# Accumulating transfers in contiguous rows, one addition of the value halves per pair of heads, and a written DMA order behind the attention

## Chip, cores and metric

The kernel runs on one core of one Trainium2 chip. The metric is the device time of one execution in microseconds. The core has a matrix engine (PE, with its own queue for weight loads, PEld), three engines for elementwise work (DVE, ACT, and the Pool, also called GpSimd), and SP, which here only issues DMAs. Each engine takes its instructions in order and waits on semaphores. An instruction that issues a DMA takes its place in the queue of the engine that issues it. All plain transfers are issued by SP (a few by ACT); those that add to their destination are issued by the Pool.

## What is computed

One hybrid decoder block with 16 meta tokens ahead of 1024 tokens of 1024 channels:

```python
h = rmsnorm(x, norm_g)
proj = jnp.einsum('bld,dn->bln', h, w_in)
u_pool, z_pool, q, k, v, z_attn, f_logit, g_pool, g_attn = jnp.split(proj, _split_points(), axis=-1)
y_pool = causal_multiscale_pool(u_pool, pool_w, pool_scale) * jax.nn.silu(z_pool)
log_f = jax.nn.log_sigmoid((f_logit + b_forget).astype(jnp.float32))
y_attn = forgetting_attention(q, k, v, log_f).reshape(B, L, ATTN_WIDTH) * jax.nn.silu(z_attn)
merged = (jax.nn.sigmoid(g_pool) * jnp.einsum('blc,cd->bld', y_pool, w_up_pool)
          + jax.nn.sigmoid(g_attn) * jnp.einsum('blc,cd->bld', y_attn, w_up_attn))
return x + jnp.einsum('bld,de->ble', merged, w_out)
```

A last RMS norm follows and the meta tokens are dropped. The pooling has four groups of 128 channels with windows of 2, 4, 8 and 16 positions. The attention has eight heads of 64 channels, is causal, and carries a decay that is summed from the forget gates.

## The kernel before, in words

Every float32 product is made from three products of rounded numbers: each operand is split into a high part (a rounded copy, written by ACT) and a low part (the rest, a subtraction on the DVE or the Pool), and high x high, high x low and low x high are added in PSUM.

**Start.** The tokens are normalised, transposed and split into `hh` and `hl`, four tensors in the pool `hp`, two for each half of the channels. They stay in SBUF until the end of product 1 below.

**Attention** (the class `Unit` and the loop over `units`, from line 777). There are 16 units: four pairs of heads, two heads each, two halves of 512 queries. A unit goes over five or nine blocks of 128 keys: products, maximum, exponent, split of the probabilities, product with the values. Heads use both halves of the 128 PSUM rows: the values' high parts give one half of 64 rows and their low parts the other, so the sum of the two halves is the result. `Unit.finish` (from line 733) copies the 128 rows to SBUF (line 737), stores the high half to `sp_y` in device memory (line 739, on SP) and adds the low half to the same place with an accumulating DMA (line 740, on the Pool). The softmax sums go to `sums` (line 745). Between these steps the PE is given filling work: the projections of queries, keys and values of the next pair, and of the gates, whose results go to device memory (line 336). The PE's order is written by hand; ACT, DVE, Pool and SP are ordered by a scheduler.

**Sums in device memory.** Two products of 1024 x 1024 matrices are made by Strassen's scheme with seven products of 512 x 512 blocks. It needs sums and differences of blocks, and these are made beside the attention by DMAs: `put` (line 578) copies, `add` (line 581) is an accumulating DMA of the Pool, behind the last sum of the softmax on that engine. `TD` are the sums for `w_out`, `GS` those for the weights of the two gates, `HS` those for the activations. `SUMS` (line 609) lists what is issued after which unit. A block has 512 rows of 512 numbers.

**The gates' products** (lines 866 to 1111). Seven products, numbered 0 to 6, of 48 matmuls each (`g_prod`, line 944; four row blocks of 12), give `za` and `zp`, the gates of the two branches. Product n needs its weights loaded (`w_in_`) and split (`w_split`, lines 929 and 931: ACT, then the Pool), and, from product 2 on, its activations loaded (`h_in`) and split (`h_split`, lines 937 to 942: ACT, then the DVE). Products 0 and 1 read `hh` and `hl` themselves; the split activations of the later ones lie in the pool `hq`, which takes over the space of `hp`. Sums of two products are made by the DVE (`plus_`, line 963) or by accumulating in the same bank. Between the products stand:

- `pool_chain` (line 865): the load of a pooling group `u` and its windowed sums on the DVE, two to five instructions; `pool_split` (line 886) splits the result; `pool_mm` (line 829) applies the 128 x 128 map.
- `sums_in` (line 893): the softmax sums are loaded, added, inverted and stored to `recs`.
- `attn_in` (line 845) loads the attention's result `y`; `attn_norm` (line 850) loads the reciprocal sums `rc`, spread over 64 rows, and multiplies.

From the first product on, the order of PE, ACT, DVE and Pool is the written one (line 980); SP is still ordered by the scheduler. The pool with tag `g` has 13 buffers of 4 KB and serves all these loads.

**Up and out.** Then the pooled and attended values are multiplied with the two up projections (32 groups of 12 matmuls, their results multiplied with the gates at line 1090), and the last Strassen product with `w_out` (line 1203) and the final norm follow.

## Time and profile before

| | us |
|---|---|
| median of three runs | 773.66 (773.03 to 774.5) |
| the profiled execution | 771.57 |
| its span | 769.8 |
| PE busy | 727.8 (95% of the span) |
| DVE busy | 538.6 (70%) |
| ACT busy | 416.9 (54%) |
| Pool busy | 352.4 (46%) |

The page of the profile gives each engine's busy time, the DMA queues, and groups of instructions by line. A row of a group names the line, the engine, the operation, the tile written and the tiles read, the count, the busy time and the mean in ns, and last the idle time of the engine just ahead of them and what ended it. The windows view gives the same busy times for a stretch of the span. The chain of waits goes back from the last instruction, at each step to what released it. In the timeline a row has start, length, engine, line and operation, and in brackets the idle time ahead and what ended it.

The stages by the trace: the attention from 26 to 487 us, the last filling work until 498.7, products 0 and 1 until 520.6, products 2 to 5 until 571.2, product 6 with the pooling maps until 599.4, the up projections until 686.4, the output product and the last norm until the end.

### The profile page before, as it was taken

The page shows a single profiled execution, that of the slowest core. Times are in us where ns is not written, and L with a number is a line of the kernel's source. Part 1 is how long each engine was busy: PE and PEld are TensorE (multiplying, and loading weights), DVE is VectorE, ACT ScalarE, POOL GpSimd, SP SyncE. Part 2 cuts the span into 40 slices and gives each one's busy share as a digit, 9 for nine tenths or more (in the row PEclk, how much of TensorE's full clock was granted, in tenths as well). Part 3 has the DMA queues.
Part 4 walks back from the last instruction along what each step waited for, and adds up shares of the span by engine and source line. Part 5 has one row for each costly group of instructions (what it writes and reads, how often), then busy time and mean ns, then how long its engine had stood idle before and what let it go on. Part 6 is the DMA issues. An engine that isn't in the chain of part 4 may idle for free.

```text
span 769.8 us, 10843 instructions
## 1 busy us (share of the span) xinstructions
PE 727.8 (95%) x3637; PEld 619.5 (80%) x3637; DVE 538.6 (70%) x913; ACT 416.9 (54%) x914; POOL 352.4 (46%) x430
## 2 busy tenths in 40 slices
PE   9999999998999989998999989999867999999996
PEld 6988989996797778887888878887755888888885
DVE  5643668697688787887878778408566744787775
ACT  7753566664676457665665466136444623535355
POOL 5422148656446585453654577347733001004343
PEclk9999999998999999999999999999997999999999
DMA  9111214957955949448373883735932547673005
GB/s 305 44 29 28 66 57 133 224 169 149 212 135 109 261 84 210 107 92 210 72 165 116 210 193 99 222 125 218 321 90 84 189 155 231 217 280 103 0 1 219
DMA packets 89866, 114.16 MB, mean 148 GB/s; under 512 B 11249, under 2 KB 54257, under 8 KB 89730
## 3 DMA queue, kind: packets, MB, share of 16 engines
q1 hardware_dynamic: 79840, 94.07, 38.7%
q0 software_dynamic: 8672, 16.78, 14.0%
q10 hardware_dynamic: 1298, 2.63, 0.9%
q8 instruction: 28, 0.46, 0.2%
q14 instruction: 28, 0.23, 0.1%
HBM read 87.04 MB, written 48.43 MB: 176 GB/s over the span
## 4 chain that ended last, share of the span: by engine, by line
PE 60%; DVE 16%; ACT 8%; issue 6%; DMA 3%; POOL 1%; POOLq 0%; SPq 0%; DVEq 0%; ACTq 0%
PE pj L164 35%; PE pj L1203 8%; PE pj L948 6%; DVE pl L714 4%; DVE S L709 2%; PE po L730 2%; PE pt L1203 2%; PE pt L948 2%; ACT S L678 2%; ACT S L710 2%; DVE m L685 1%; PE ps L669 1%; PE ps L670 1%; DMA hraw<-hs 1%; ACT ph L713 1%
## 5 line engine op out<-in xcount | busy, mean ns | idle before, releaser
L164 PE MATMUL pj<-hh,whi 128*128 128x512 f32 (+3 forms) x640 | 146.4, 356 | 0.4 <-DVE V L304 0.4
L164 PE MATMUL pj<-hl,whi 128*128 128x512 f32 (+3 forms) x640 | 145.1, 356 | 0.0
L164 PE MATMUL pj<-hh,wlo 128*128 128x512 f32 (+3 forms) x640 | 144.1, 352 | 0.0
L152 POOL TENSOR_TENSOR wlo<-raw,whi 128x256 fp32r<-128x256 f32 x116 | 94.9, 941 | 97.5 <-ACT whi L150 48.0
L164 PEld LDWEIGHTS pj<-hl,whi 128*128 128x128 f32 x640 | 110.7, 193 | 12.5
L164 PEld LDWEIGHTS pj<-hh,whi 128*128 128x128 f32 x640 | 109.5, 191 | 12.4 <-PE pj L294 0.6
L164 PEld LDWEIGHTS pj<-hh,wlo 128*128 128x128 f32 x640 | 108.9, 190 | 11.7
L714 DVE TENSOR_TENSOR pl<-S,ph 128x512 fp32r<-128x512 f32 (+4 forms) x112 | 98.1, 888 | 22.4 <-ACT ph L713 21.5
L722 POOL TENSOR_TENSOR acc<-acc,S 128x272 f32<-128x272 f32 (+4 forms) x80 | 77.7, 971 | 8.4 <-ACT S L710 2.8
L678 ACT ACTIVATE S<-ps,negc 128x400 f32<-128x400 f32 (+2 forms) x96 | 48.5, 514 | 57.4 <-DVE S L676 52.6
L685 DVE TENSOR_TENSOR m<-m,S 128x272 f32<-128x272 f32 (+4 forms) x80 | 52.4, 655 | 23.2 <-ACT S L678 21.1
L136 POOL TENSOR_TENSOR gw<-graw,gw 128x256 fp32r<-128x256 f32 x48 | 48.5, 1065 | 28.9 <-ACT gw L929 28.9
L710 ACT ACTIVATE S<-S 128x512 f32<-128x512 f32 (+4 forms) x112 | 49.2, 478 | 19.6 <-DVE S L709 19.5
L948 PE MATMUL pj<-gh,gw 128*128 128x512 f32 x180 | 45.0, 403 | 13.8 <-DVE zp L963 10.0
L713 ACT ACTIVATE ph<-S 128x512 fp32r<-128x512 f32 (+4 forms) x112 | 52.0, 478 | 4.4 <-PE po L730 4.1
L948 PEld LDWEIGHTS pj<-gh,gw 128*128 128x128 f32 x180 | 34.4, 194 | 23.4 <-issue 10.4
L709 DVE TENSOR_TENSOR S<-S,pt 128x512 f32<-128x512 f32 (+4 forms) x112 | 50.7, 498 | 0.6
L669 PE MATMUL ps<-qa,ka 128*128 128x512 f32 (+4 forms) x112 | 38.0, 340 | 9.9 <-ACT S L678 9.9
L730 PE MATMUL po<-pl,V 128*128 128x512 f32 (+4 forms) x112 | 38.6, 345 | 7.4 <-DVE pl L714 6.8
L1090 DVE TENSOR_TENSOR rl<-pj,rl 128x512 f32<-128x512 f32 x32 | 22.0, 690 | 30.4 <-PE pj L164 30.4
L150 ACT ACTIVATE whi<-raw 128x512 fp32r<-128x512 f32 x58 | 33.9, 622 | 14.0 <-PE pj L164 7.6
L720 POOL TENSOR_TENSOR acc<-S 128x400 f32<-128x400 f32 (+1 forms) x16 | 20.2, 1266 | 39.0 <-ACT S L710 39.0
(227 smaller groups left out, 1351.7 us busy)
## 6 DMA issues: line engine op xcount, KB each, us to landing
raw<-in_w_in_dram SPq DMA_DIRECT2D x31, 512.0 KB, 5.9
xt<-in_x_dram SPq DMA_DIRECT2D x8, 512.0 KB, 6.4
sp_gp<-st SPq DMA_DIRECT2D x16, 256.0 KB, 4.2
gs<-in_w_in_dram POOLq DMA_DIRECT2D x4, 1024.0 KB, 10.1
td<-in_w_out_dram POOLq DMA_DIRECT2D x4, 1024.0 KB, 12.1
sp_ga<-st SPq DMA_DIRECT2D x16, 256.0 KB, 2.7
graw<-gs SPq DMA_DIRECT2D x8, 512.0 KB, 5.2
rl<-sp_gp SPq DMA_DIRECT2D x8, 512.0 KB, 4.2
```

The source lines that it names most:

```text
L152: ins = nc.gpsimd.tensor_tensor(lo[:, k:k + 2], raw[:, k:k + 2], r32(hi[:, k:k + 2]), op=ALU.subtract)
L164: nc.tensor.matmul(ps, a, b, start=(i == 0), stop=(i == len(seq) - 1))
L678: nc.scalar.activation(s[:kb, f0:], ps[:kb, f0:], AF.Identity, bias=nb_)
L685: nc.vector.tensor_tensor(m[:kb, c0:], m[:kb, c0:], s[:kb, c0:], op=ALU.max)
L709: nc.vector.tensor_tensor(s[:kb, c0:], s[:kb, c0:], self.pm[:kb, c0:], op=ALU.subtract)
L710: exps.append(nc.scalar.activation(s[:kb, c0:], s[:kb, c0:], AF.Exp))
L713: nc.scalar.activation(ph[:kb, c0:], s[:kb, c0:], AF.Copy)
L714: dves.append(nc.vector.tensor_tensor(pl[:kb, c0:], s[:kb, c0:], r32(ph[:kb, c0:]), op=ALU.subtract))
L722: accs.append(nc.gpsimd.tensor_tensor(acc[:kb, c0:], acc[:kb, c0:], s[:kb, c0:], op=ALU.add))
L730: nc.tensor.matmul(self.po[:, c0:], v, r[:kb, c0:], start=(b == 0 and i == 0), stop=(b == self.nb - 1 and i == 1))
L948: nc.tensor.matmul(ps, op_w[n][p][k // 2][:, k % 2, i * 128:(i + 1) * 128], op_h[n][q][k // 2][:, k % 2], start=start and m == 0, stop=m = ...
L1203: nc.tensor.matmul(ps, pick(A_, k, p)[:, i * 128:(i + 1) * 128], pick(B_, k, q)[:, c0:c1], start=start and n == 0, stop=n == 11, skip_grou ...
```

## The change

Four things are changed.

1. **Form of the additions.** An accumulating transfer of a block goes as 128 rows of 2048 numbers (8 KB) between contiguous blocks in place of 512 rows of 512 (2 KB). So that both sides are contiguous blocks of device memory, the low parts of `hl` and the second summands in the weights are first copied there (`l11`, `l22`, `GS[5]`, `TD[5]`), and the list `SUMS` is written anew. It has 14 accumulating transfers as before, and 15 plain entries (four of them for the blocks of `hh` and `hl`) in place of 11.
2. **Value halves.** A unit stores both halves, to `sp_y` and `sp_y2`. `add_y(p)` adds the two blocks of a pair of heads with one accumulating transfer. It is issued after units 5, 9 and 13 for the first three pairs, and behind the attention for the last.
3. **Order behind the attention.** From product 0 on, SP's order too is the written one. The loads get functions of their own (`u_in`, `rc_in`, `sums_in` parted from `sums_out`) and stand earlier. The chains of groups 2 and 1 stand ahead of product 1, that of group 0 between the first sums behind it; `h_split(2)` and `h_split(3)` stand together; `attn_norm(0)` and `(1)` come together, the other two a product earlier each. A tile of 4 KB that is never read is added to the pool `hq`.
4. **One part of a split on the DVE.** In `w_split` for products 3 to 6 the last of the four subtractions is made by the DVE.

The core of the diff:

```diff
     def add(dst, src):
-        after(nc.gpsimd.dma_start(dst, src, accum_op=ALU.add), accs[-1])
+        d, r = [t.rearrange("(p k) c -> p (k c)", k=4) for t in (dst, src)]
+        after(nc.gpsimd.dma_start(d, r, accum_op=ALU.add, max_dma_last_dim=8192), accs[-1])
...
     def put_h(n):
         put(rows_of(HS[n]), hblock(hh4, n))
-
-    def add_h(n):
-        add(rows_of(HS[n]), hblock(hl4, n))
+        put(rows_of(HS["l" + n]), hblock(hl4, n))
...
+    def add_y(p):
+        d, r = [spill[n, p].rearrange("(p k) c -> p (k c)", k=2) for n in ("y", "y2")]
+        after(nc.gpsimd.dma_start(d, r, accum_op=ALU.add, max_dma_last_dim=8192), accs[-1])
...
-            yd = spill["y", self.p][hr, self.q0:self.q0 + 512]
-            nc.sync.dma_start(yd, t[hr])
-            after(nc.gpsimd.dma_start(yd, t[lr], accum_op=ALU.add), accs[-1])
+            for n, part in (("y", hr), ("y2", lr)):
+                nc.sync.dma_start(spill[n, self.p][hr, self.q0:self.q0 + 512], t[part])
...
         sums_of(i)
+        if i % 4 == 1 and i > 1:
+            add_y(i // 4 - 1)
...
+    def rc_in(p):
+        RC[p] = rc = gp.tile([128, SEQ], F32, name="rc", tag="g")
         for e in range(2):
...
+    def attn_norm(p):
+        nc.vector.tensor_tensor(Y[p], Y[p], RC[p], op=ALU.mult)
...
-            pool_tt(lo[k][:, c], raw_w[n][k][:, c], r32(hi[k][:, c]), ALU.subtract)
+            tt(lo[k][:, c], raw_w[n][k][:, c], r32(hi[k][:, c]), ALU.subtract,
+               nc.vector if n > 2 and k and c else nc.gpsimd)
...
+    add_y(3)
     w_in_(1)
-    next(cg[3])
+    u_in(3)
     h_in(2)
     w_in_(2)
+    u_in(2)
     for k in range(2):
         w_split(1, k)
-    run(cg[3])
+    run(pool_chain(3))
     M2 = ExitStack()
-    M2.enter_context(tc.manual_schedule(engines={mybir.EngineType.PE, mybir.EngineType.Activation,
-                                                 mybir.EngineType.DVE, mybir.EngineType.Pool}))
+    M2.enter_context(tc.manual_schedule())
+    sums_in()
     prods(ga_, 0, True)
+    u_in(1)
+    u_in(0)
     h_in(3)
+    sums_out()
...
     w_in_(3)
-    sums_in()
+    run(pool_chain(2))
+    run(pool_chain(1))
     prods(gb_, 1, True)
     HX.close()
...
-    h_split(2)
-    next(cg[2])
-    next(cg[2])
-    plus_(za[0][:, T0_], gb_[0])
-    next(cg[2])
-    plus_(za[1][:, T0_], gb_[1])
-    run(cg[2])
-    plus_(za[2][:, T0_], gb_[2])
     attn_in(0)
     attn_in(1)
+    rc_in(0)
+    h_split(2)
+    h_split(3)
+    c0_ = pool_chain(0)
+    for i in range(3):
+        plus_(za[i][:, T0_], gb_[i])
+        next(c0_, None)
+    w_in_(4)
+    hq.tile([128, SEQ], F32, name="pad", bufs=1)
+    h_in(4)
+    rc_in(1)
+    attn_in(2)
+    attn_in(3)
 
     prods(ga_, 2, False)
-    h_split(3)
     for k in range(2):
         w_split(3, k)
     plus_(za[3][:, T0_], gb_[3])
-    w_in_(4)
-    h_in(4)
-    run(cg[1])
+    w_in_(5)
+    h_in(5)
     for i in range(4):
         keep(zp[i][:, T0_], ga_[i])
     attn_norm(0)
-    attn_in(2)
+    attn_norm(1)
+    rc_in(2)
+    rc_in(3)
```

Behind products 3 and 4 the loads `w_in_(6)` and `h_in(6)` go one product earlier, chain 0 leaves its place behind product 3, `attn_norm(2)` and `(3)` go one product earlier, and `pool_split` and the first step of chains 0 to 2 lose a written dependency on an earlier instruction of the same engine.

More of the change, by code (lines that the diff above doesn't have):

```diff
@@ L137, in pool_tt, with tt @@
         return ins
+    def tt(out, x, y, op, eng):
+        if eng is nc.gpsimd:
+            pool_tt(out, x, y, op)
+        else:
+            eng.tensor_tensor(out, x, y, op=op)
     los = []
@@ L875, in pool_chain @@
             add = nc.vector.tensor_tensor(n[:, lo + step:], s[:, lo + step:], s[:, lo:L - step], op=ALU.add)
-            if not i:
+            if g == 3 and not i:
                 after(add, last_dve)
@@ L1022, in tile_hybrid_block @@
     h_split(4)
-    w_in_(5)
-    h_in(5)
+    w_in_(6)
+    h_in(6)
     pool_split(3)
@@ L1028, in tile_hybrid_block @@
     pool_split(2)
-    run(cg[0])
     keep(zp[2][:, T1_], gb_[2])
     keep(zp[3][:, T1_], gb_[3])
-    attn_norm(1)
-    attn_in(3)
+    attn_norm(2)
     prods(gb_, 4, False)
@@ L1038, in tile_hybrid_block @@
     h_split(5)
-    w_in_(6)
-    h_in(6)
     pool_split(1)
@@ L1044, in tile_hybrid_block @@
         silu(zp[i][:, T0_], zp[i][:, T0_], -1.0)
-    attn_norm(2)
+    attn_norm(3)
     prods(ga_, 5, False, (3, 2, 1, 0))
```

75 lines of the change are left out of this document (36 added, 39 removed).

## The prediction

> **What bounds the kernel now.** I read the page first, then the windows cut at the borders of the stages, then the chain of waits from 500 to 600 us, then who waited for whom in that stretch. The page and the DMA view:
>
> ```profile
> span 769.8 us, 10843 instructions
> DMA packets 89866, 114.16 MB, mean 148 GB/s; under 512 B 11249, under 2 KB 54257, under 8 KB 89730
> sp_y<-t SPq DMA_DIRECT2D x16, 128.0 KB, 3.2
> ```
>
> The windows (first pair: length and PE busy, the last three: granted clock, DMA share, GB/s):
>
> ```profile
> core 0: us, PE busy (x) PEld busy (x) DVE busy (x) ACT busy (x) POOL busy (x), PEclk, DMA share, GB/s
> 26.00:487.00 461.00, 442.88 (x2354) 386.24 (x2353) 349.31 (x655) 273.16 (x679) 246.03 (x288) 0.99 0.55 132
> 487.00:520.60 33.60, 33.60 (x150) 27.69 (x149) 4.83 (x6) 8.86 (x12) 12.09 (x17) 1.00 0.58 187
> 520.60:571.00 50.40, 45.52 (x193) 35.45 (x192) 37.10 (x32) 26.84 (x32) 34.45 (x29) 1.00 0.70 230
> 571.00:599.40 28.40, 18.39 (x74) 14.68 (x73) 17.09 (x22) 13.82 (x22) 9.19 (x12) 0.82 0.32 99
> 599.40:686.40 87.00, 87.00 (x385) 72.03 (x384) 55.07 (x82) 35.19 (x49) 5.72 (x8) 1.00 0.64 216
> ```
>
> The kernel is bound by the PE nearly everywhere, so a change can only pay where the PE stands still. In the attention that is 461.0 - 442.9 = 18.1 us, spread over 16 units. From 599.4 to 686.4 it is nothing. Between 520.6 and 599.4 it is 4.9 + 10.0 = 14.9 us in a sixth of the attention's time, and this is the stage that the change rewrites. Ahead of it, from 487 to 520.6, the PE is full while the DVE works 4.8 us of 33.6. The chain through the stage (start, length, what):
>
> ```profile
> 509.84 8.16 PE pj L948 x36
> 518.00 2.73 PE pt L948 x12
> ...
> 571.19 1.39 PE pj L164 x6
> 572.86 3.96 DMA rc<-recs
> ...
> 578.04 0.69 DVE zp L963
> 578.75 1.82 ACT zp L960 x3
> 581.13 0.69 DVE wlu L1069
> 581.82 0.61 DVE zp L963
> 582.57 4.39 PE pj L948 x12
> ...
> 588.35 2.74 PE pj L948 x12
> ```
>
> An undisturbed product of 48 matmuls takes 8.16 + 2.73 = 10.9 us. Products 2 to 5 start at 520.7 and end at 571.2: 50.5 us where 4 x 10.9 = 43.6 would do, so 6.9 us go in small waits. Then the PE runs six matmuls of the pooling map (1.39 us) and stands from 572.6 to 582.6, since product 6 adds to a bank that the DVE reads last at L963. In that gap an add of L963, queued on the DVE behind a normalisation waiting for `rc`, comes at 578.0, and a second one ends at 582.4. The 12 matmuls after the gap take 4.39 us, the next 12 take 2.74: 1.65 us more. So the stage holds 6.9 + 10.0 + 1.65 = 18.6 us above the PE's own work.
>
> The DVE is what it waits for. Its waits from 487 to 600 us (total, times, longest), and its groups from 520.6 to 600:
>
> ```profile
> DVE gh L940 <- ACT gh L937: 21.4, 2, 12.2
> DVE y L855 <- DMA rc<-recs: 9.4, 2, 7.2
> DVE y L855 <- DMA y<-sp_y: 2.4, 1, 2.4
> ```
>
> ```profile
> L942 DVE TENSOR_TENSOR gh<-hraw,gh 128x1024 fp32r<-128x1024 f32 x8 | 11.2, 1446 | 2.3 <-ACT gh L937 2.3
> L890 DVE TENSOR_TENSOR pll<-u,plh 128x1024 fp32r<-128x1024 f32 x4 | 6.2, 1562 | 1.6 <-ACT plh L889 1.6
> ...
> L882 DVE SCALAR_TENSOR_TENSOR u<-s,u 128x1024 f32<-128x1024 f32 x3 | 4.5, 1501 | 0.1
> L875 DVE TENSOR_TENSOR s<-u 128x1039 f32<-128x1039 f32 x3 | 4.2, 1411 | 0.0
> ...
> L875 DVE TENSOR_TENSOR s<-s 128x1037 f32<-128x1037 f32 x2 | 2.8, 1422 | 0.1
> ...
> L875 DVE TENSOR_TENSOR s<-s 128x1033 f32<-128x1033 f32 x1 | 1.2, 1225 | 0.0
> ```
>
> It stands 21.4 us for `gh` of product 2, then has all pool chains but one (12.7 us) in the crowded part, and there waits another 11.8 us for `rc` and `y` transfers. The SP row says why they come late:
>
> ```profile
> 538.55 1.12 SPq L854 DMA_DIRECT2D rc<-recs  x2
> ```
>
> **The change part by part.**
>
> *Pool chains 2 and 1 ahead of product 1, chain 0 between the first sums.* Three chains are nine instructions, 4.5 + 4.2 + 2.8 + 1.2 = 12.7 us. Chain 0 is one L875 and one L882, 1.41 + 1.50 = 2.9 us. The other seven, chains 2 and 1, move into the 21.4 us in which the DVE stood: 9.8 us. Their loads (`u_in`) stand ahead of h_in(3) on SP and land while the PE is full. Cover: products 0 and 1, 21.8 us long. Chain 0 stays past 520, but ahead of the work that was late.
>
> *h_split(2) and (3) together, with a padding tile.* Eight tiles of the pool `hq` lie on the space of the transposed activations; the pad is meant to put them on the half that product 0 reads (8 x 4,096 bytes fit in two tensors of 17,408, if they start at the same byte). If so, their low parts (one left of h_split(2), two of h_split(3) at 1.45) run during product 1 too: about 4.3 us more out of the crowded part. If not, they wait for product 1 as now; with chains 2 and 1 out of the way that costs the PE under 1 us.
>
> *rc and y loads.* The store of `recs` is followed by the loads y0, y1, rc0 and only then by w_in_(4), where SP stands until product 1 has left the space; behind that stand h_in(4), rc1, y2, y3. So rc0 goes out before product 1 is over, the rest right behind it, where the first two loads of `rc` now go out at 538.6; attn_norm(0) stands behind the last low part and six short instructions, about 525 by the sums above. I take the 11.8 us of DVE waiting as gone; if rc1 (behind two loads of 1 MB) is late by 4 us, that lies under product 2, which ends at 531.6.
>
> *Four parts of w_split from the Pool to the DVE.* A 128x512 addition is 0.69 us (L963 above): 2.8 us more on the DVE. On the Pool, the splits of products 3 to 6:
>
> ```profile
> 501.31 8.40 POOL L136 TENSOR_TENSOR gw<-graw,gw 128x256 fp32r<-128x256 f32 x12 [2.04 <-ACT gw L929]
> ```
>
> ```profile
> L136 POOL TENSOR_TENSOR gw<-graw,gw 128x256 fp32r<-128x256 f32 x16 | 11.5, 811 | 2.0 <-ACT gw L929 2.0
> L740 POOL DMA_DIRECT2D sp_y<-t x1 | 0.8, 842 | 11.3 <-DMA sp_y<-t 11.3
> L136 POOL TENSOR_TENSOR gw<-graw,gw 128x256 fp32r<-128x256 f32 x32 | 37.0, 1192 | 26.8 <-ACT gw L929 26.8
> ```
>
> (The first fence is the Pool's timeline; in the second the first two rows are of 487 to 520.6, the third of 520.6 to 600.) Six instead of eight at 1.19 us are 7.2 us per product of 10.9, so the Pool keeps up. The moved chains now run beside the first group: at worst its 16 become 1192 ns each, 6 us later, ending near 516 instead of 501.3 + 8.4 = 509.7 and still ahead of product 2.
>
> *add_y(3)* is the one wait that is new on the Pool. Behind it stand the splits of product 1. But the accumulating transfer in its place now already makes the Pool wait 11.3 us, for a store of the same unit: no change.
>
> The DVE so gains 9.8 + 4.3 + 11.8 - 2.8 = 23.1 us, more than the 14.9 the PE lost: something else is late next. For products 2 to 5 I find nothing, since their splits wait for the product two before. They end at 520.7 + 43.6 = 564.3, the six matmuls at 565.7. For product 6 it is the ACT and DVE pair that starts when product 4 leaves its tiles, at 520.7 + 32.7 = 553.4. The ACT rows for it:
>
> ```profile
> 566.72 1.99 ACT L937 ACTIVATE gh<-hraw 128x1024 fp32r<-128x1024 f32 x2
> ...
> 572.07 1.04 ACT L889 ACTIVATE plh<-u 128x1024 fp32r<-128x1024 f32 x1
> ...
> 580.49 0.61 ACT L1068 ACTIVATE whu<-rawu 128x512 fp32r<-128x512 f32 x1
> ```
>
> Weights' high part, as large as gh's, 1.99 and gh 1.99: 557.4; the second low part 1.9 later (two of 1.45, the first starting a microsecond before that): 559.3; add 0.69, silu 0.61 (1.82 for three): 560.6; plh 1.04, pll 1.56: 563.2; three adds 2.07, last silu 0.61, whu 0.61, wlu 0.69, last add 0.69: 567.9. The PE waits 567.9 - 565.7 = 2.2 us there, not 10.0. Product 6 starts at 567.9 instead of 582.6: 14.7 us. To this comes the 1.65 us after the gap, between 0 (a 2.2 us gap also slows what follows) and 1.65; I take all of it. By the Trainium skill (TensorE: Matmul & The Clock Gate, section "What's actually happening") the clock halves after an idle window of about 3.4 us and returns after a busy one; by that rule 2.2 us is too short and the 1.65 is saved, and the trace agrees with it at the 10.0 us gap.
>
> *The transfers in the attention.* 16 accumulating issues of a unit's value half become 16 plain stores on SP and four additions of a pair; 14 other additions stay 14, in 128 rows of 8 KB instead of 512 of 2 KB. The rows of the Pool's issues:
>
> ```profile
> L740 POOL DMA_DIRECT2D sp_y<-t x16 | 13.8, 863 | 16.9 <-DMA sp_y<-t 11.8 <-ACT ph L713 5.1
> ...
> L582 POOL DMA_DIRECT2D gs<-in_w_in_dram x4 | 4.8, 1189 | 0.5 <-issue 0.2 <-PE po L730 0.2
> ```
>
> An issue costs 0.86 us with 64 rows and 1.19 with 512, so one of 128 rows lies between; near the first, 0.9. The Pool's issues go from 13.8 + 14 x 1.19 = 30.5 to 18 x 0.9 = 16 us. Traffic rises by some 6.3 MB of 114 (four more copies of a block of 1.05 MB, and the second halves stored, 2.1). No PE wait in the attention leads to the Pool or to a DMA, so I price this at 0, between -18.1 (all of the idle time) and a loss as in the third rival.
>
> Sum: 14.7 + 1.65 = 16.4 us. The profiled execution took 771.57 us, 1.8 around its span of 769.8; the median of the runs is 773.66. So 755.2 for a profiled execution, 757.3 for the median.
>
> **Rivals.** *The DVE stays late for products 2 to 5.* What speaks for it: its two-input instructions stretch beside the Pool (1446 ns for L942; 1225 for the shortest L875 of like size). Then the 6.9 us of small waits stay and only the gap shrinks, 7.8 + 1.65 = 9.5 us: 764.2. Against it: 23.1 us of relief. The Trainium skill (SBUF — State Buffer, section "SBUF: two separate sides") holds that a VectorE instruction with two SBUF inputs and a GpSimd instruction exclude each other for their whole length; by this both engines' work would add up, which is this rival, and the 811 against 1192 ns of the Pool's splits goes its way.
>
> *The attention gains as well.* The Pool issues 14 us less; if a quarter of the 18.1 us of PE idle time goes with it, 4.5 us: 752.8. Against it: no wait of the PE names it.
>
> *The attention loses.* Place: the SP queue there, whose order the scheduler sets anew. Each unit has one more store; weight loads queue behind. If the landing of one, 3.2 us, is exposed in a unit, the gain is gone from five units on (5 x 3.2 = 16); in eight of 16 it is 25.6 - 16.4: 9 us slower, 782.9. Against it: DMA share 0.55 there.
>
> *It does not do what it says:* loads find no free buffer, SP in written order stands where it stood, and the DVE's waits only change names: 773.7.
>
> **How the numbers follow.** My forecast (754.5 to 760) has 0.58, the late DVE 0.20, the gaining attention 0.14, the losing one 0.05, no effect 0.03. Faster is 0.92, same 0.03, slower 0.05, a measurement of this kernel telling 0.2% from nothing. The range of 752 to 766 holds the forecast, most of the late DVE and half of the gaining attention.
>
> **What would show it.** Right: PE idle time from 520.6 on under 5 us up to the pooling products, no clock under 0.95 there, chains 2 and 1 before product 2, no wait of L855 for `rc`, the attention's 461 us within 2 us. Wrong: low parts of `gh` still releasing the PE (the late DVE), SP standing over 10 us on a load that the next product needs, or the end of the attention moved.

## The result and the profile after

The changed kernel took 744.17 us (median of four runs, 743.1 to 746.76) beside 773.88 for the kernel before (773.03 to 774.5): a ratio of 0.9622, 95% interval 0.9595 to 0.9648. The forecast was 757.3, with a range of 752 to 766. Its direction was right; the gain was 29.7 us instead of 16.4, and the time lies outside the range. The profiled execution took 744.3 us.

The page of the profile after, where it answers to the lines shown of before:

```profile
span 742.6 us, 10841 instructions
DMA packets 88906, 120.45 MB, mean 162 GB/s; under 512 B 11377, under 2 KB 54385, under 8 KB 86786
q0 software_dynamic: 2336, 16.78, 12.2%
```

The traffic grew by 6.3 MB, as worked out. The queue of the accumulating transfers, q0 (packets, MB, share), carries the same bytes as before, in 2336 packets instead of 8672. To find the place of the gain I cut both spans where product 0 begins (498.66 before, 486.15 after) and where the up projections begin (599.21 and 572.51). Windows of before, then of after (columns as in the prediction):

```profile
26.00:498.66 472.66, 454.54 (x2405) 395.86 (x2404) 352.35 (x658) 275.30 (x682) 249.10 (x293) 0.99 0.56 136
498.66:599.21 100.55, 85.67 (x362) 68.01 (x360) 55.80 (x56) 47.19 (x63) 52.66 (x53) 0.95 0.51 167
```

```profile
474.50:508.00 33.50, 33.50 (x149) 27.62 (x148) 27.16 (x21) 12.75 (x17) 14.95 (x17) 1.00 0.71 237
508.00:551.60 43.60, 43.60 (x194) 36.08 (x194) 28.36 (x24) 26.09 (x35) 29.91 (x24) 1.00 0.68 211
551.60:572.50 20.90, 18.30 (x73) 14.55 (x72) 13.28 (x19) 10.21 (x17) 6.62 (x8) 0.92 0.33 106
572.50:659.50 87.00, 87.00 (x385) 72.05 (x384) 55.39 (x82) 35.33 (x49) 5.76 (x8) 1.00 0.65 219
26.00:486.15 460.15, 449.08 (x2420) 392.44 (x2419) 346.84 (x663) 276.81 (x684) 239.22 (x287) 1.00 0.58 154
486.15:572.51 86.36, 83.76 (x361) 68.62 (x360) 59.60 (x57) 45.96 (x62) 46.05 (x42) 0.98 0.59 192
```

The gates' products went from 100.55 to 86.36 us: 14.2 us. The stretch ahead of them went from 472.66 to 460.15: 12.5 us, where I had put zero. What follows took 170.6 and 170.1 us. Together 27.2 us, which is the difference of the spans. Within the 12.5 us the PE's idle time fell from 18.1 to 11.1 us, and its busy time from 454.5 to 449.1, although 15 more matmuls fell into the second window (2420 against 2405), as the PE ran less often at a lower granted clock (0.99 against 1.00).

Who the PE waits for, after: first in the gates' products (480 to 600 us), then in the attention; the third fence is the attention before (total, times, longest).

```profile
PE pj L967 <- DVE zp L982: 2.6, 1, 2.6
```

```profile
PE ps L680 <- ACT S L689: 7.5, 11, 1.9
PE po L741 <- DVE pl L725: 2.6, 3, 1.5
```

```profile
PE ps L669 <- ACT S L678: 9.9, 14, 2.1
PE po L730 <- DVE pl L714: 6.8, 3, 3.8
```

In the products one wait is left, the gap ahead of product 6. In the attention the waits kept their names and lost 6.6 us. The order of the instructions on PE and DVE in the attention is the same in both kernels; on ACT one exponent has another place, and what differs besides are the Pool's issues, the place of a few of its subtractions, and SP. So something makes the same DVE instructions slower before. It shows in single instructions. The DVE's subtractions and maxima of two tiles in SBUF take 0.2 to 1.3 us as a rule (median 0.69). In the attention before, seven of them take over 2.3 us, 27.5 us in sum; after, five, 18.7 us. One of before, with the Pool and the PE (timelines: start, length, instruction):

```profile
284.23 1.29 POOL L582 DMA_DIRECT2D hsB<-hs  x1
285.04 3.27 POOL L152 TENSOR_TENSOR wlo<-raw,whi 128x256 fp32r<-128x256 f32 x4
284.72 4.03 DVE L714 TENSOR_TENSOR pl<-S,ph 128x400 fp32r<-128x400 f32 x1
288.80 0.45 PE L730 MATMUL po<-pl,V 128*128 128x400 f32 x1 [1.71 <-DVE pl L714]
```

And one that is left after:

```profile
274.83 0.81 POOL L590 DMA_DIRECT2D td<-td  x1
275.39 3.07 POOL L158 TENSOR_TENSOR wlo<-raw,whi 128x256 fp32r<-128x256 f32 x4
275.36 5.04 DVE L725 TENSOR_TENSOR pl<-S,ph 128x512 fp32r<-128x512 f32 x1 [0.16 <-ACT ph L724]
```

All twelve lie so: the Pool issues an accumulating transfer, goes on without a pause to a run of subtractions (or of softmax sums), and a DVE instruction that begins then ends within 0.6 us of the end of the Pool's run. I shall call it held, and say that the engine that goes on meanwhile has the turn.

**Theory A:** an issue by the Pool, with additions of the Pool right behind it, takes the turn from the DVE until the run is over; the change has fewer such issues (18 instead of 30) at other places. **Rival B:** the traffic of the accumulating transfers slows the DVE or the loads; contiguous rows made it lighter. **Rival C:** the order behind the attention reaches back into it. (In the expectations below a "Theory C" is another: chance, since any moved issue shifts which DVE instruction is hit.)

### The profile page after: what moved, and what is told of

Its sections match the earlier page's. It is cut to its first block, busy times and chain, and to the rows that moved or that the text cites. A ratio compares the mean times of both kernels' runs of the same rounds, so it can differ in the third digit from the quotient of the medians.

```text
span 742.6 us, 10841 instructions
## 1 busy us (share of the span) xinstructions
PE 720.2 (97%) x3637; PEld 616.6 (83%) x3637; DVE 536.5 (72%) x917; ACT 417.0 (56%) x914; POOL 334.4 (45%) x410
## 3 DMA queue, kind: packets, MB, share of 16 engines
q0 software_dynamic: 2336, 16.78, 12.2%
## 4 chain that ended last, share of the span: by engine, by line
PE 71%; DVE 9%; ACT 8%; issue 4%; DMA 1%; POOL 0%; POOLq 0%; DVEq 0%; ACTq 0%; SPq 0%
PE pj L170 45%; PE pj L1227 8%; PE pj L967 6%; PE po L741 4%; PE pt L1227 2%; DVE pl L725 2%; PE pt L967 2%; PE ps L680 2%; ACT S L689 2%; PE ps L681 2%; ACT S L721 1%; ACT ph L724 1%; PE pj L515 1%; DVE m L696 1%; ACT whi L156 1%
## 5 line engine op out<-in xcount | busy, mean ns | idle before, releaser
L170 PE MATMUL pj<-hl,whi 128*128 128x512 f32 (+3 forms) x640 | 142.7, 352 | 0.0
L158 POOL TENSOR_TENSOR wlo<-raw,whi 128x256 fp32r<-128x256 f32 x116 | 91.7, 871 | 97.9 <-ACT whi L156 41.5
L170 PEld LDWEIGHTS pj<-hl,whi 128*128 128x128 f32 x640 | 108.9, 190 | 12.0
L170 PEld LDWEIGHTS pj<-hh,whi 128*128 128x128 f32 x640 | 108.8, 190 | 11.8
L170 PEld LDWEIGHTS pj<-hh,wlo 128*128 128x128 f32 x640 | 108.6, 190 | 11.5
L725 DVE TENSOR_TENSOR pl<-S,ph 128x512 fp32r<-128x512 f32 (+4 forms) x112 | 89.3, 811 | 21.2 <-ACT ph L724 20.8
L733 POOL TENSOR_TENSOR acc<-acc,S 128x272 f32<-128x272 f32 (+4 forms) x80 | 76.7, 959 | 12.5 <-ACT S L721 6.6
L696 DVE TENSOR_TENSOR m<-m,S 128x272 f32<-128x272 f32 (+4 forms) x80 | 47.6, 595 | 21.1 <-ACT S L689 18.9
L136 POOL TENSOR_TENSOR gw<-graw,gw 128x256 fp32r<-128x256 f32 x40 | 44.3, 1187 | 23.5 <-ACT gw L947 14.6
L967 PEld LDWEIGHTS pj<-gh,gw 128*128 128x128 f32 x180 | 34.9, 194 | 10.5 <-issue 3.0
```

The lines of the kernel that those rows point to most:

```text
L158: ins = nc.gpsimd.tensor_tensor(lo[:, k:k + 2], raw[:, k:k + 2], r32(hi[:, k:k + 2]), op=ALU.subtract)
L170: nc.tensor.matmul(ps, a, b, start=(i == 0), stop=(i == len(seq) - 1))
L696: nc.vector.tensor_tensor(m[:kb, c0:], m[:kb, c0:], s[:kb, c0:], op=ALU.max)
L725: dves.append(nc.vector.tensor_tensor(pl[:kb, c0:], s[:kb, c0:], r32(ph[:kb, c0:]), op=ALU.subtract))
L733: accs.append(nc.gpsimd.tensor_tensor(acc[:kb, c0:], acc[:kb, c0:], s[:kb, c0:], op=ALU.add))
L967: nc.tensor.matmul(ps, op_w[n][p][k // 2][:, k % 2, i * 128:(i + 1) * 128], op_h[n][q][k // 2][:, k % 2], start=start and m == 0, stop=m = ...
```

## The experiments

All times are medians; the ratios are to runs of the kernel before on the same chip. The last column is read from the one profiled execution. That of e7 (738.4) and that of e11 (737.13) were the shortest of their kernels, that of e14 (748.16) the longest.

| run | us | ratio, 95% interval | product 0 at |
|---|---|---|---|
| kernel before | 773.88 | | 498.66 |
| changed kernel | 744.17 | 0.9622 (0.9595 to 0.9648) | 486.15 |
| e1 order alone | 755.25 | 0.9786 (0.9754 to 0.9818) | 497.70 |
| e2 rows alone | 770.24 | 0.9977 (0.9956 to 0.9998) | 494.57 |
| e3 halves alone | 768.07 | 0.9933 (0.9903 to 0.9963) | 496.45 |
| e4 rows and halves | 760.87 | 0.9855 (0.9819 to 0.9891) | 487.14 |
| e6 memsets (misplaced) | 754.45 | 0.9761 (0.9724 to 0.9797) | 495.58 |
| e7 addition first | 742.63 | 0.9609 (0.9569 to 0.9649) | 483.99 |
| e8 no additions | 733.23 | 0.9489 (0.9461 to 0.9517) | 477.83 |
| e9 small additions | 742.14 | 0.9621 (0.9592 to 0.965) | 485.31 |
| e10 plain copies | 733.45 | 0.9511 (0.9484 to 0.9537) | 475.79 |
| e11 issues between sums | 742.91 | 0.9635 (0.9603 to 0.9667) | 482.65 |
| e14 pauses | 743.54 | 0.9624 (0.9586 to 0.9661) | 490.49 |

**e1, the order alone.** The changed kernel with parts 1 and 2 of the change taken back:

```diff
-        d, r = [t.rearrange("(p k) c -> p (k c)", k=4) for t in (dst, src)]
-        after(nc.gpsimd.dma_start(d, r, accum_op=ALU.add, max_dma_last_dim=8192), accs[-1])
+        after(nc.gpsimd.dma_start(dst, src, accum_op=ALU.add), accs[-1])
...
-            for n, part in (("y", hr), ("y2", lr)):
-                nc.sync.dma_start(spill[n, self.p][hr, self.q0:self.q0 + 512], t[part])
+            yd = spill["y", self.p][hr, self.q0:self.q0 + 512]
+            nc.sync.dma_start(yd, t[hr])
+            after(nc.gpsimd.dma_start(yd, t[lr], accum_op=ALU.add), accs[-1])
```

> Only the written order behind the attention, the pad and the split on the DVE; additions and value halves as before. From product 0 on the changed kernel was 14.2 us shorter, up to product 0 12.5 us. If the two parts do not depend on each other: product 0 starts at 498.7 within 1 us as before, the stage from there to the up projections takes 86.4 us, and the time is 773.9 - 14.5 = 759.4. Rival (the attention gains because the scheduler or the buffers behind it are set anew): product 0 starts earlier, time under 753.

The PE's only wait in its gates' products, and their window:

```profile
PE pj L961 <- DVE zp L976: 2.4, 1, 2.4
497.70:583.87 86.17, 83.77 (x361) 68.65 (x360) 56.73 (x56) 47.42 (x64) 45.46 (x44) 0.98 0.58 186
```

It gains 17.1 us (expected 14.5); the stage is as long as in the changed kernel (86.17 against 86.36), product 0 begins only 1 us earlier than before, and the seven held instructions are there. So rival C falls: the order gives the stage's part alone, and the attention's gain comes from parts 1 and 2.

**e2, e3, e4: rows alone, halves alone, both.** The kernel before, with the hunks of `add`, `put_h` and `SUMS`; with those of `finish` and `add_y`; with both sets.

> Only the additions in 128 rows of 8 KB between contiguous blocks with their list; value halves and the order behind the attention as before. Theory A (a Pool that comes late from an accumulating issue runs its additions one behind the other, and a DVE instruction with two SBUF inputs stands still for that long): five of the seven DVE instructions of over 2.5 us in the kernel before overlap or follow a block addition, so most of the 12.5 us come with this part: 8 to 10 us, 764 to 766. Theory B (less DMA work, fewer packets): about the same size, but the DVE's long instructions stay. Theory C (chance: any moved issue shifts which DVE instruction is hit): anything between -6 and +6 us.

> Only the value halves stored twice and added once per pair of heads; 16 issues of 0.86 us on the Pool become four. Theory A: one of the seven long DVE instructions overlaps such an issue, 2 to 4 us: 770 to 772. Theory B: more bytes, so no gain: 773 to 775. Theory C: between -6 and +6 us.

> Both changes of the attention, the stage behind it as before. All theories but the rival of the first run: product 0 starts 12.5 us earlier as in the changed kernel, 773.9 - 12.5 = 761.4. If rows alone and halves alone do not add up to this within 2 us, that speaks for C.

Rows give 2.1 us, halves 4.3 (5.3 without the longest of the ten runs of e3, which spread over 13 us), both 11.5, as expected for both. The two parts do not add up, though with these intervals not by much more than the noise, and my expectation of 8 to 10 us from the rows failed. With either alone, six and five instructions stay held (23.3 and 21.4 us), at other places than before; with both, five (18.6 us) at nearly the places of the changed kernel. Which issue meets a DVE instruction on the PE's path is a matter of position, and a shift of one issue moves the rest. By e4's own words this speaks for its Theory C, chance of position; it does not speak against A, which says what an issue does to an instruction that it meets. What does add up is attention and order: 11.5 + 17.1 = 28.6 of the 29.7 us.

**e5, the two engines by themselves.** A small program: the DVE adds 128x512 tiles, the Pool subtracts 128x256 tiles, alone, together, and behind issues.

> Only the disputed cost; it computes none of the block. Eight DVE additions of 128x512 with two SBUF inputs (tile dvesb) stand alone, beside eight and beside four Pool subtractions of 128x256 (poolsb) one behind the other, and beside eight with a memset of one column between them; then eight DVE additions of a PSUM and an SBUF input (dveps) and eight DVE transposes (dvetr) beside eight on the Pool; then DVE additions beside an accumulating transfer in 512 and in 128 rows, without and with four Pool subtractions behind it. Theory A (the Pool's run holds off a two-input DVE instruction until it ends): alone 685 ns each; beside a run one of them takes about the length of the run, 0.7 us for each Pool instruction, 5 us beside eight and 3 us beside four; with the memsets between, or with one SBUF input, none over 1.5 us. Theory B (the DMA traffic matters): the long ones come beside the transfer and not beside the Pool's run.

Alone a DVE addition takes 0.69 us and a subtraction of the Pool 0.72. Together they take turns, 1.21 and 1.17 us each, however long the Pool's run is: Theory A as I had it, that any run holds the DVE, fell. DVE instructions with one input in PSUM (0.68) and transposes (0.67) don't notice the Pool. Beside an issue without a run the DVE stays at 0.69. But one addition, begun 0.22 us after an issue with four subtractions behind it, took 3.94 us, up to the end of the run. So A was narrowed: a run behind an issue. The turns agree with the Trainium skill (SBUF — State Buffer, section "SBUF: two separate sides"), by which such a pair excludes each other for the length of an instruction; that one engine then keeps the turn for a whole run does not follow from it.

**e6, memsets behind the splits.** The changed kernel with one line more in the weights' split:

```diff
             ins = nc.gpsimd.tensor_tensor(lo[:, k:k + 2], raw[:, k:k + 2], r32(hi[:, k:k + 2]), op=ALU.subtract)
+            nc.gpsimd.memset(gapz, 0.0)
```

> The changed kernel with a memset of one column on the Pool behind each subtraction of a weight's split (116 of about 0.1 us). Theory A: the DVE gets through at each of them, no two-input instruction of over 2.5 us is left in the attention, and its 9.6 us of PE gaps fall to 5 or less: 738 to 742. If a memset does not open the way: 744 to 746, as 12 us more on a Pool that is half idle. Theory C (chance): anything within 5 us of 744.

It tested nothing. The memsets depend on nothing, and the scheduler put all 116 into the program's first 40 us. There the start is changed with them and 8.4 us are lost; between the splits of the attention there is none, and the held instructions stayed. e14 does it again.

**e7, the running addition first.** The remaining gap ahead of product 6 waits for a `zp` addition that stands behind a weight's split on the DVE:

```diff
-    ws[0, 0] = up_weights(0, 0)
     plus_(zp[0][:, T1_], ga_[0])
+    ws[0, 0] = up_weights(0, 0)
```

> The changed kernel with the last addition that product 6 waits for ahead of the first up weights' low part on the DVE (two lines changed places). The PE's gap ahead of product 6 is 2.6 us; the addition there stands behind a DVE instruction that waits for ACT (0.61 + 0.69 us). The gap falls to about 1.3 us. If the 12 slow matmuls behind it (4.58 us against 2.92) come from the length of the gap, they go too: 3 us, 741. If any gap slows them: 1.3 us, 743.

The first 12 matmuls of product 6 there:

```profile
551.46 2.97 PE L967 MATMUL pj<-gh,gw 128*128 128x512 f32 x12 [0.50 <-ACT zp L979]
483.99:566.65 82.66, 82.16 (x361) 67.48 (x360) 59.35 (x56) 45.68 (x62) 43.14 (x41) 1.00 0.61 198
```

The stage is 3.7 us shorter: 2.1 from the gap (0.5 instead of 2.6) and 1.6 because the matmuls behind it keep the full clock (2.97 us for 12). In the median, 742.63 against 744.17, the intervals overlap; and the swap alone doesn't secure it, since in e14, which has it too, the gap was 2.2 us again.

**e8, e9, e10: issue or traffic.** The changed kernel without the 18 accumulating transfers; with them, but 16 numbers a row instead of all; with plain copies of the same bytes issued by SP in their place:

```diff
# e8, in add and add_y
-        after(nc.gpsimd.dma_start(d, r, accum_op=ALU.add, max_dma_last_dim=8192), accs[-1])
+        pass
# e9, in add (add_y alike)
-        d, r = [t.rearrange("(p k) c -> p (k c)", k=4) for t in (dst, src)]
+        d, r = [t.rearrange("(p k) c -> p (k c)", k=4)[:, :16] for t in (dst, src)]
# e10, in add and add_y
-        after(nc.gpsimd.dma_start(d, r, accum_op=ALU.add, max_dma_last_dim=8192), accs[-1])
+        after(nc.sync.dma_start(d, r), stores[-1])
```

> The changed kernel without its 18 accumulating transfers: the sums stay unmade, the rest is as it is. What the Pool's issues still cost in the attention: three of the five long DVE instructions left there follow one directly. Theory A: the runs of four splits behind them come earlier and hit other instructions or none: 0 to 5 us less, 739 to 744. Theory B: the attention gets shorter by the traffic that goes, also 0 to 5 us, but with the long DVE instructions still there.

> The changed kernel with its 18 accumulating transfers cut to 16 numbers of each of their rows (the sums stay unmade but for those). The issues on the Pool stay where they are, the traffic of the additions goes (16.8 MB). Theory A, as it stands now (a DVE instruction with two SBUF inputs that comes during or right behind an accumulating issue gets no turn until the Pool's run behind that issue ends): the long DVE instructions stay, product 0 starts near 486, 742 to 746. Theory B (the traffic): as without additions, product 0 near 478, 733 to 736.

> The changed kernel with plain copies on SP in place of its 18 accumulating transfers, same rows, same places (the sums stay unmade). No accumulating issue on the Pool, nearly all of the traffic. Theory A: no DVE instruction over 2.5 us, product 0 near 478, 732 to 737. Theory B: product 0 near 484 to 486, 741 to 745.

The place of 275 us again, in e9 and in e10 (each the Pool, then the DVE):

```profile
273.41 0.81 POOL L590 DMA_DIRECT2D td<-td  x1
273.93 5.04 DVE L725 TENSOR_TENSOR pl<-S,ph 128x512 fp32r<-128x512 f32 x1 [0.16 <-PE po L741]
```

```profile
268.45 1.89 POOL L604 TENSOR_TENSOR neg<-neg,hl 128x256 f32<-128x256 f32 x2
269.02 0.71 DVE L725 TENSOR_TENSOR pl<-S,ph 128x512 fp32r<-128x512 f32 x1 [0.16 <-ACT ph L724]
26.00:475.79 449.79, 445.05 (x2409) 391.40 (x2407) 333.99 (x665) 277.63 (x684) 229.81 (x266) 1.00 0.52 158
```

Without the traffic but with the issues (e9) six instructions stay held, the same 5.04 us among them, and the time is that of the changed kernel. With the traffic but without issues by the Pool (e10) none is held in the whole attention, the same instruction takes 0.71 us, product 0 begins at 475.79, and the time is that of e8. Rival B falls, Theory A holds. It also prices what the changed kernel still pays: some 11 us (744.17 against 733.2 and 733.5), or 9 to 10 by the ratios. That is twice what the expectation of e8 gave to any theory.

**e11, issues between the softmax sums.** The addition is issued between two running sums of the next unit, with e7's swap:

```diff
-            fn(*args)
+            if fn is add:
+                pend.append((fn, args))
+            else:
+                fn(*args)
...
+            if b in (2, 3) and pend:
+                fn, args = pend.pop(0)
+                fn(*args)
```

> The changed kernel with the additions put on the Pool between two of its running sums of the next unit, each of which waits for ACT, in place of the end of a unit, where splits stand behind them; and the last addition ahead of product 6 put first, as in an earlier run. Theory A: the run behind an issue is one or two sums, not four to eight splits, so the long DVE instructions go or halve; product 0 near 479 to 482, 734 to 739. Theory B: product 0 near 486, 741 to 744. Theory C: either way by up to 6 us.

Missed: 742.91, no better than e7. Five instructions are held at new places, since splits and sums run behind the issue there too. Two of them are copies with one input, in SBUF (`m<-S`, 4.05 and 6.30 us), so it is not only instructions with two inputs that can be held.

**e12, e13, e15: the hold by itself.** e12 repeats e5's case: runs of four without an issue; issues alone; an issue and four; an issue and eight; an issue in 512 rows and four.

> The cost by itself, repeated; it computes none of the block. DVE additions with two SBUF inputs run without a break; the Pool does, at shifting moments: runs of four subtractions (10 times), one accumulating issue of 128 rows alone (10), the issue with four (10) and with eight (6) subtractions behind it, and an issue of 512 rows with four (6). Theory A: no DVE instruction over 1.3 us in the first two parts; in the third some of about 4 us, in the fourth some of about 7 us, as long as the run; in the fifth as in the third.

One beat of its third part: the Pool, and the DVE's group in that time (count, busy, mean ns):

```profile
146.26 0.93 POOL L86 DMA_DIRECT2D dst<-db  x1
146.83 3.14 POOL L57 TENSOR_TENSOR poolsb<-go,y 128x256 f32<-128x256 f32 x4
L42 DVE TENSOR_TENSOR dvesb<-go,y 128x512 f32<-128x512 f32 x2 | 7.7, 3907 | 0.0
```

No addition over 1.21 us in ten plain runs, none over 0.70 beside ten issues alone. Behind an issue, one of 3.4 to 4.0 us at nine of ten runs of four, and of 6.0 to 6.8 at five of six runs of eight: there the hold is as long as the run. At the other two the engines took turns in spite of the issue. Behind an issue in 512 rows one addition was held at all six runs (2.3 to 3.6 us), but only the first until the run's end; the other five ended 2.8 us before it, and the two engines then took turns.

e13 asked what ends it, in a steady row of beats.

> A program by itself: the DVE adds 128x512 pairs of SBUF tiles without a break, the Pool does one beat after another, eight beats in each of six parts, and nothing of the reference is computed. Parts: an accumulating transfer issued and four subtractions behind it; the same with a memset of one number between the issue and the run; the same with a memset behind each subtraction; a plain (not accumulating) transfer issued by the Pool and four subtractions; an accumulating issue, an addition of one number that waits for an ACT copy, and four subtractions; four subtractions and then the issue. Theory A (the issue leaves the Pool one instruction ahead, so that its next one always asks before the DVE does, until the run ends or the Pool has to wait): a DVE addition of 3.6 to 4.0 us in nearly every beat of the first and of the fourth part, none over 1.7 us in the fifth and the sixth; in the second and third it is open whether a memset ends it, 1.2 us if it does. Rival (only the accumulation does it): the fourth part shows 1.2 us. Rival (it is a matter of which engine happens to start first, the issue being only a delay): some held additions in the fifth and sixth parts too.

It was inconclusive. In its first and last parts the DVE kept the turn until its own row was over, so that no later beat met it (the last section shows this). A memset behind the issue changed nothing (8 of 8 held, 2.4 to 3.7 us), a memset behind each subtraction seemed to help (1 of 8 held), a plain transfer issued by the Pool held 1 of 8. The fifth part, where Theory A expected no hold, had 8 of 8 (2.5 to 3.8 us), but it did not try a wait: the ACT copy was always done before the Pool's addition came. In both parts most of these holds ended before the run did. In these steady rows a beat inherits its turn from the beat before, and the first beats of the four parts in the middle were all held. So e15 has single runs, each meeting the DVE at another moment, and e14 the memsets in the kernel, kept in place:

```diff
+    def pause(ins):
...
+        m = nc.gpsimd.memset(gapz[:, :1], 0.0)
+        after(m, ins)
+        return m
...
+            if gap:
+                after(ins, gap)
+            gap = pause(ins)
```

> The changed kernel with the running addition ahead of the weights' split at the end of the gates' products (as in the seventh run), and in the attention a memset of one number behind every low-part split and every subtraction of a negated block on the Pool, kept in its place (in the sixth run the scheduler had put them all at the start). The program by itself showed held additions in 1 of 8 beats with such memsets, but that one was the first, in which the DVE had had the engine's turn to itself; in the attention every issue meets the DVE like that. If the memset frees the DVE: held instructions gone or two at most, the attention some 6 to 8 us shorter, 733 to 737 us. If only its place in a steady row of beats made the difference: five held instructions as in the changed kernel, 741 to 744 us (129 memsets of 0.1 us on the Pool cost the PE nothing).

> A program by itself, nothing of the reference is computed: the DVE repeats two additions of SBUF tiles and one transpose; the Pool, every 6 us and each time at another moment of the DVE's row, does one of five things, eight times each: four subtractions; an accumulating issue and four; the same with a memset of one number behind each; a plain issue and four; an accumulating issue, a memset of 128x1024 numbers (about 1 us) and four. Theory A (the issue is what puts the Pool ahead): no addition over 1.7 us in the first part, 3 us or more in most of the second; the fourth tells whether accumulation is needed, the third and fifth what ends it. Rival (only the moment decides in which the Pool's run begins, with an issue or without): held additions in the first part as often as in the second, at certain moments only.

e15, one beat each of its first part (no issue), its second (accumulating) and its fourth (plain issue by the Pool); the Pool, then the DVE's two additions, whose sum is shown:

```profile
16.64 4.64 POOL L57 TENSOR_TENSOR poolsb<-go,y 128x256 f32<-128x256 f32 x4
16.58 1.79 DVE L42 TENSOR_TENSOR dvesb<-go,y 128x512 f32<-128x512 f32 x2
...
113.16 0.82 POOL L88 DMA_DIRECT2D dst<-db  x1
113.73 3.02 POOL L57 TENSOR_TENSOR poolsb<-go,y 128x256 f32<-128x256 f32 x4
113.72 4.19 DVE L42 TENSOR_TENSOR dvesb<-go,y 128x512 f32<-128x512 f32 x2
...
281.83 0.54 POOL L86 DMA_DIRECT2D dst<-db  x1
282.38 2.77 POOL L57 TENSOR_TENSOR poolsb<-go,y 128x256 f32<-128x256 f32 x4
282.38 3.92 DVE L42 TENSOR_TENSOR dvesb<-go,y 128x512 f32<-128x512 f32 x2
```

Without an issue 0 of 8 are held (longest 1.22 us); with an accumulating one 8 of 8 (3.0 to 3.6); with memsets behind each subtraction 8 of 8; with a plain issue 8 of 8 (2.75 to 3.3); with a memset of 1.2 us behind the issue 8 of 8. All 32 were held until the run's end. At the eight moments tried in each part the moment of meeting made no difference, nor did the addition in the transfer: what parts the first row from the others is the issue on the Pool's queue. e14 agrees, at the same place of the attention:

```profile
278.82 0.81 POOL L600 DMA_DIRECT2D td<-td  x1
279.39 1.01 POOL L167 TENSOR_TENSOR wlo<-raw,whi 128x256 fp32r<-128x256 f32 x1
280.07 0.36 POOL L151 MEMSET lead<- 128x1 f32 x1
279.36 5.22 DVE L738 TENSOR_TENSOR pl<-S,ph 128x512 fp32r<-128x512 f32 x1 [0.16 <-PE po L754]
```

The memset stands between the splits, the DVE is held for 5.22 us all the same, and the median is e7's. Four instructions of the attention are held there, against five in the changed kernel. The traces of the kernels bear it out too: of the splits and maxima that began amid a run of the Pool, with at least two of the run still to start, 28 in the changed kernel and 39 in e10 had no issue at the run's head, the longest of them 1.53 us; the four that had one took 2.9 to 4.2.

What stays open is why the issue has this effect, why it sometimes has none (two runs of e12, most beats in two parts of e13), and what gives the turn back before the run's end (the last part of e12, two parts of e13). No version that makes all the sums clearly beat the changed kernel.

## Why the prediction was right in direction and wrong in size

**The gates' products: mechanism right, two terms wrong.** Forecast 14.7 us from an earlier product 6 and 1.65 from the clock; measured 14.2 in all.

- *Products 2 to 5 without a wait.* Right: 43.5 us (508.05 to 551.57), forecast 43.6, no wait of the PE. The pad seems to do what I supposed, since the four high parts are written while product 1 runs, which ends at 508.0; no run leaves the pad out:

```profile
497.86 3.89 ACT L956 ACTIVATE gh<-hraw 128x1024 fp32r<-128x1024 f32 x4
```

- *`rc` and `y` no longer late.* Wrong in size and of no price: of the 11.8 us that I took as gone, 10.5 us of waiting for `rc` are still there. The second `rc` comes 8.2 us late, forecast 4, but both waits lie under products.

```profile
DVE y L871 <- DMA rc<-recs: 10.5, 2, 8.2
```

- *A gap of 2.2 us ahead of product 6.* Right: 2.6. From the start of product 0 to that of product 6 it is 69.6 us instead of 83.9: 14.3 us, forecast 14.7.
- *The 1.65 us behind the gap.* Wrong. The first 12 matmuls still take 4.58 us, the next 12 2.92:

```profile
555.72 4.58 PE L967 MATMUL pj<-gh,gw 128*128 128x512 f32 x12 [2.60 <-DVE zp L982]
561.53 2.92 PE L967 MATMUL pj<-gh,gw 128*128 128x512 f32 x12
```

I took the upper bound because of the rule of about 3.4 us in the Trainium skill (TensorE: Matmul & The Clock Gate, section "What's actually happening"). Here half clock follows a gap of 2.6 us, in e1 one of 2.4, and in e7 it does not follow one of 0.5; the measurement decides. The length of the gap is not all that counts. The 12 matmuls behind the same gap in e9, then in e10, and the window of e10 in which the granted clock is half (0.50):

```profile
554.73 3.00 PE L967 MATMUL pj<-gh,gw 128*128 128x512 f32 x12 [2.45 <-DVE zp L982]
545.17 4.53 PE L967 MATMUL pj<-gh,gw 128*128 128x512 f32 x12 [2.42 <-DVE zp L982]
546.27:549.69 3.42, 3.42 (x10) 2.64 (x9) 0.08 (x1) 0.71 (x2) 2.80 (x4) 0.50 0.00 0
```

So the 1.65 us could come either way at a gap of this size (the last section says more), and the forecast had no ground to take all of it.

**The attention: this is the step that failed.** "No PE wait in the attention leads to the Pool or to a DMA, so I price this at 0". It gained 12.5 us, and of the signs that I had named, "the attention's 461 us within 2 us" failed. The bounds of this term, down to -18.1 us, held what came, but the range of the forecast did not carry them: it went by the rival in which the attention gains, which had a quarter of the idle time, 4.5 us. The sentence is true of the view and false as an argument. The view of waits names the last instruction in the chain, a DVE split or an ACT exponent; it doesn't say why that one was late. A held instruction waits for no semaphore: it stands in the trace as busy. The group's mean, 888 ns for `pl` before, hid a few of 4 us among 112. The prediction had what it took to look there, since it cited the 811 and 1192 ns of the Pool's splits and held that the two engines can exclude each other; but it used this only for the stage behind the attention. It was also one-sided about the issues: their time on the Pool fell from 30.9 to 15.7 us, much as forecast (30.5 to 16), rows of which are

```profile
L618 POOL DMA_DIRECT2D sp_y<-sp_y x4 | 4.0, 999 | 9.3 <-DVE fin L922 9.3
L590 POOL DMA_DIRECT2D td<-td x4 | 3.3, 823 | 0.4 <-issue 0.2
```

but it was asked only what they cost the Pool, and not what they do to its neighbour. And the idle time was no bound for the gain: 5.5 of the 12.5 us came off the PE's busy time, from matmuls that ran at the full clock again. The paragraph on `add_y(3)` saw no change either; a pooling sum behind that issue is held for 6.90 us, though under a full PE and so at no price.

**The rivals.** The late DVE (764.2) did not come: products 2 to 5 had no wait. The losing attention had the wrong sign. The gaining attention had the right one, with a chance of 0.14, but a third of the size and another road: it let the Pool's shorter issues give back idle time, where the runs show held DVE instructions. That the change doesn't do what it says is refuted by e1 and e4, each of which gains by its own part.

## What to carry to other kernels

Before an engine is called off the path, look for single instructions of its neighbours that are several times longer than their group's mean, and for what the other engines did at that moment: in these traces the wait for a shared turn is booked as busy time, and the view of waits cannot name it. On this chip, as these runs show it, a transfer issued by the Pool ahead of a run of its additions mostly costs the DVE instruction with two inputs in SBUF that meets it the whole run (32 of 32 single runs in e15, 14 of 16 behind issues in 128 rows in e12, none of 18 without an issue; in two of e13's steady rows only the first beat). Issue from SP what can be issued there, and count such issues by what runs behind them, not by their own length. A short PE gap can cost more than itself: 2.6 us of waiting cost 4.3 here, and 2.45 us in e9 cost next to nothing more.

## What the runs showed of the hardware that was not expected

- The turn can stay with the other side as well. In e13, whose DVE row had no pause, the first of four subtractions behind an accumulating issue stood for 26.53 us (the row shows it with the second, 0.71), and an addition of one number on the Pool for 60.50 us, until the DVE's 110 additions were over:

```profile
27.05 27.21 POOL L57 TENSOR_TENSOR poolsb<-go,y 128x256 f32<-128x256 f32 x2
387.83 60.50 POOL L75 TENSOR_TENSOR z<-q,y 128x1 f32<-128x1 f32 x1 [43.32 <-ACT q L74]
```

- Half clock mostly followed the PE's gaps of 2.2 to 2.6 us ahead of product 6. In the attention it followed one of 1.1 us before and one of 1.97 in e14, but none of the five between 0.9 and 1.95 us in the changed kernel. Two things more can be read from the granted clock in the traces. It changes on a fixed grid: half clock began at 100.87, 186.21, 363.70 and 575.33 us in the kernel before, 25, 52 and 62 steps of 3.41 us apart, and lasted one, two, one and three steps. And it followed a step in which the PE stood idle for long in sum: from 26 us on, in the thirteen traces of the kernel and its versions, never for under 1.47 us, always for over 1.74, and sometimes for what lies between. In e10 2.31 us of the gap ahead of product 6 fell into one step; in e9 a border of the grid parted the gap into 1.67 and 0.78, and the clock stayed full. So where a gap lies on the grid counts as well as how long it is; no run moved a gap on purpose.
- An accumulating issue of 128 rows between blocks mostly took 0.81 us (the first 1.08), a little less than one of 64 rows from SBUF before (0.86), and one of 512 rows 1.05 to 1.6.
